# Between the heads and the MLP: the last block's projected outputs copied by ScalarE, and three row pairs' latent products ahead of the context

## The chip, the cores and the metric

One core of a Trainium2 chip. The metric is the device time of one execution in microseconds, as the median of several runs. All tensors are fp32 in HBM.

## What is computed

The reference is a two-layer diffusion trunk over 256 context and 1024 latent tokens of width 1024. Layer 0 mixes tokens with multi-head latent attention (MLA), layer 1 with gated linear attention (GLA). Cut to what matters here:

```python
y_lat = o_lat @ w_o                                   # projected heads (and y_ctx in layer 0)
x_lat = x_lat + m_lat[:, 2] * rms_norm(y_lat, g1)     # sandwich norm, residual
h     = modulate(rms_norm(x_lat, g2), m_lat[:, 3], m_lat[:, 4])
x_lat = x_lat + m_lat[:, 5] * rms_norm(square(relu(h @ w1)) @ w2, g3)
# in layer 0 the same for x_ctx, with its own modulation
```

The stretch of interest lies between `@ w_o` and the first products of `h @ w1`.

## The kernel before

The tokens are handled in three blocks: block 0 is the context (256 tokens), blocks 1 and 2 are the latents (512 each). The order of the blocks is `BLK_ORDER = (1, 0, 2)`, so block 2 is the last to get its projection. Activations lie transposed, 128 features by 512 (or 256) tokens in a tile, eight tiles for a block.

Each fp32 product is made of three rounded products. A factor is split into a high part, cast by ScalarE (ACT, L203), and a low part, source minus high part, mostly by VectorE (DVE, L200). The matmul of a pair of tiles is then high by high (L233), high by low (L234), low by high (L235). So nothing on TensorE (PE) can start before an ACT cast, nor its second matmul before a DVE subtraction.

`out_items` projects the heads of one block: two halves of four PSUM tiles; each tile is copied to SBUF (L809) and its square is summed (`sumsq`: square on ACT, L297 or L300; sum on DVE, L301). `residual_norm_steps` then makes the norm: `rstd` sums over the partitions with a matmul by ones (L308), does L314 to L316 on ACT and L317 to L319 on DVE; each tile is scaled (L857), the old stream, loaded by DMA, is added (L859), the sum is stored (L865) and its square summed; a second `rstd` follows, and then the modulated tiles (L877/L878 for latents; L325 on DVE, L327 on ACT as the high part, L328 on DVE as the low part for the context).

`mlp` multiplies by `w1` in a Strassen-like scheme. For a pair `p` of its row strips, `up_first` loads, casts and splits two weight tiles and makes two 4-step products with block 1's tiles (24 matmuls of 128x512; copy L971, sum L886, L965 and L966). `up_first_ctx` makes the context's two up-products for the same pair (24 matmuls of 128x256 each; the first with the two weights held from `up_first`, the second with two weights of its own; then L936 and L937). In layer 0 `PLAN["ahead"]` pairs get their `up_first` before the first `up_first_ctx`. The weights come out of a pool of 12 tiles (`w`), so three pairs of two weights, high and low, fill it.

Each engine's order is not the order of the code: a scheduler with a timeline of its own orders the instructions of the whole program, and every engine works its own queue off in that order. The ends of all this that matter here are the order rows under "The change".

Of the kernel before, what the change touches and what calls it, by code (L numbers as in the profile page):

```python
# [35 lines left out]
BLK_ORDER = (1, 0, 2)  # L36
# [43 lines left out]
           7: []},  # L80
 'pbufs': {'m': 56, 'c': 16, 'w': 12, 'stg': 12, 's': 4, 't': 7},
 'early': [8, 11],
 'ahead': 2,
 'etick': [10.0, 5.0],
 'fill': [[2, 1], [2, 1], [1, 1], [1, 1], [1, 1], [1, 1], [1, 1], [1, 1], [1, 0], [1, 0], [1, 0], [1, 0], [1, 0],
          [1, 0], [1, 1], [2, 1], [2, 2], [2, 2], [2, 2], [2, 3], [2, 2]],
# [21 lines left out]
class Trunk:  # L108
# [684 lines left out]
    def out_items(self, res, l, b, wname, src, off, xsrc):  # L793
        t0, w = BLK[b]
        acc = self.m(512)[:, :w]
        o, ys = [], []
        for half in range(2):
            pss = [self.ps(w) for _ in range(4)]
            for k in range(KT):
                if half == 0:  # L800
                    o.append(self.msplit(self.load(src[k, :, t0 - off:t0 - off + w]), w, self.nc.vector))
                ww = self.weight(self.I[wname][k * P:(k + 1) * P, half * 512:half * 512 + 512], self.nc.vector)
                for n in range(4):
                    self.mm3(pss[n], self.cols(ww, n * P), o[k], k == 0, k == KT - 1)
                self.tick(w * PLAN["tk"][0])
                yield
            for n in range(4):
                y = self.m(512)[:, :w]
                self.nc.vector.tensor_copy(y, pss[n])  # L809
                self.sumsq(acc, pss[n], half == 0 and n == 0, w)  # L810
                ys.append(y)
        self.bg.append(self.residual_norm_steps(res, l, b, ys, acc, xsrc, 2, (l, 4), (l, 3), b != 0))
# [870 lines left out]
```

## Time and profile before

| | |
|---|---|
| median of 3 runs | 2874.68 us (2873.05 to 2877.36) |
| the profiled execution | 2872.26 us, span of its trace 2870.5 us |
| mean granted TensorE clock | 0.98 of full speed |
| PE busy | 2747.0 us (96%) |
| DVE busy | 2280.4 us (79%) |
| ACT busy | 1594.9 us (56%) |

How to read it: the span is what the trace covers; the execution's own time is 1.8 us longer, and the median of the runs is 2.42 us above the profiled execution. An engine's row of a timeline gives the start in us from the span's start, the time in us, the line, the operation and its tiles; "x4" is a run of four; in brackets stands how long the engine had been idle before it and what released it. Runs of one engine overlap a little, as the next instruction begins before the last has drained.

### The profile page before, as it was taken

How to read it: one execution, taken by the hardware profiler on the slowest of the kernel's cores; microseconds unless marked ns; L12 is line 12 of the kernel's file. 1: busy time of each engine (PE TensorE's matmuls, PEld its weight loads, DVE VectorE, ACT ScalarE, POOL GpSimd, SP SyncE). 2: the span in 40 equal slices, each digit the busy share in tenths (PEclk: the TensorE clock that was granted, in tenths of full speed). 3: DMA queues.
4: the chain of work that ended last, by engine and by line, in shares of the span. 5: the costliest groups of instructions: out<-in, count | busy, mean ns of one | idle time of the engine just before them, and what ended most of it. 6: DMA issues, size and time to landing. Idle time of an engine off the chain costs nothing.

```text
span 2870.5 us, 44551 instructions
## 1 busy us (share of the span) xinstructions
PE 2747.0 (96%) x14774; PEld 2362.8 (82%) x14774; DVE 2280.4 (79%) x4303; ACT 1594.9 (56%) x3341; POOL 638.2 (22%) x464
## 2 busy tenths in 40 slices
PE   8999898999989999999999999999888999999997
PEld 6788887898779888888888888888786778888877
DVE  6898899887788887798868674476998998777766
ACT  4667576666566444444545456666655645554443
POOL 2554444422000000000002232566560000000022
PEclk9999999999999999999999999999999999999999
DMA  7122334323637675498745566776675767577454
GB/s 251 43 79 67 122 108 132 101 78 120 217 118 236 197 253 180 152 342 283 255 125 187 164 202 191 243 241 213 209 257 198 235 212 247 191 278 254 149 178 154
DMA packets 319529, 535.50 MB, mean 187 GB/s; under 512 B 33217, under 2 KB 96577, under 8 KB 319297
## 3 DMA queue, kind: packets, MB, share of 16 engines
q1 hardware_dynamic: 313472, 527.40, 55.6%
q10 hardware_dynamic: 5760, 5.25, 0.5%
q8 instruction: 116, 1.90, 0.3%
q14 instruction: 117, 0.95, 0.1%
q0 software_dynamic: 64, 0.00, 0.0%
HBM read 412.19 MB, written 120.32 MB: 186 GB/s over the span
## 4 chain that ended last, share of the span: by engine, by line
PE 75%; DVE 14%; ACT 4%; DMA 4%; issue 2%; POOL 1%; SPq 0%; DVEq 0%; ACTq 0%; POOLq 0%
PE ps L234 23%; PE ps L233 23%; PE ps L235 22%; DVE m L200 2%; PE ps L736 1%; DVE y L709 1%; DVE ada L252 1%; DMA stg<-hid 1%; PE ps L704 1%; ACT m L203 1%; PE ps L705 1%; PE ps L706 1%; PE ps L707 1%; PE ps L708 1%; PE ps L308 1%
## 5 line engine op out<-in xcount | busy, mean ns | idle before, releaser
L234 PE MATMUL ps<-m,w 128*128 128x512 f32 (+1 forms) x2320 | 895.8, 387 | 12.1 <-DVE m L200 11.4
L233 PE MATMUL ps<-m,w 128*128 128x512 f32 (+1 forms) x2320 | 880.7, 389 | 19.4 <-ACT m L203 15.3
L235 PE MATMUL ps<-m,w 128*128 128x512 f32 (+1 forms) x2320 | 887.9, 386 | 2.1 <-DVE w L200 2.1
L200 POOL TENSOR_TENSOR w<-stg,w 128x512 fp32r<-128x512 f32 (+2 forms) x138 | 197.6, 1435 | 1696.2 <-ACT w L203 1622.7
L233 PEld LDWEIGHTS ps<-m,w 128*128 128x128 f32 x2320 | 438.2, 190 | 111.9 <-ACT m L203 23.1
L234 PEld LDWEIGHTS ps<-m,w 128*128 128x128 f32 x2320 | 440.6, 190 | 104.3 <-DVE m L200 18.2
L235 PEld LDWEIGHTS ps<-m,w 128*128 128x128 f32 x2320 | 438.6, 190 | 90.9 <-DVE w L200 4.3
L203 ACT CAST w<-stg 128x512 fp32r<-128x512 f32 (+2 forms) x510 | 312.1, 616 | 318.2 <-PE ps L234 250.9
L200 DVE TENSOR_TENSOR w<-stg,w 128x512 fp32r<-128x512 f32 x372 | 273.2, 737 | 120.5 <-ACT w L203 109.6
L203 ACT CAST m<-stg 128x512 fp32r<-128x512 f32 x296 | 177.5, 625 | 142.5 <-DMA stg<-hid 127.0
L200 DVE TENSOR_TENSOR m<-stg,m 128x512 fp32r<-128x512 f32 x244 | 167.5, 699 | 47.9 <-ACT m L203 47.0
L234 PE MATMUL ps<-m,m 128*128 128x256 f32 (+1 forms) x632 | 197.3, 312 | 6.3 <-DVE m L200 4.0
L233 PE MATMUL ps<-m,m 128*128 128x256 f32 (+1 forms) x632 | 189.2, 316 | 13.0 <-DVE m L1531 6.8
L233 PE MATMUL ps<-c,w 128*128 128x256 f32 (+1 forms) x664 | 189.5, 289 | 12.3 <-ACT c L327 4.6
L235 PE MATMUL ps<-m,m 128*128 128x256 f32 (+1 forms) x632 | 193.6, 306 | 0.0
L234 PE MATMUL ps<-c,w 128*128 128x256 f32 (+1 forms) x664 | 187.4, 284 | 1.3 <-DVE c L432 1.3
L235 PE MATMUL ps<-c,w 128*128 128x256 f32 (+1 forms) x664 | 186.2, 285 | 0.0
L203 ACT CAST w<-m 128x512 fp32r<-128x512 f32 x128 | 79.2, 622 | 116.9 <-PE ps L234 116.7
L233 PEld LDWEIGHTS ps<-m,m 128*128 128x128 f32 x632 | 124.1, 198 | 22.6 <-DVE m L1531 7.7
L233 PEld LDWEIGHTS ps<-c,w 128*128 128x128 f32 x664 | 127.3, 193 | 17.4 <-ACT c L327 5.0
L886 DVE TENSOR_TENSOR t<-ps,t 128x512 f32<-128x512 f32 x164 | 111.0, 684 | 37.5 <-PE ps L235 31.6
L965 ACT ACTIVATE t<-t 128x512 f32<-128x512 f32 x109 | 68.7, 631 | 127.0 <-DVE t L886 120.2
(301 smaller groups left out, 5826.9 us busy)
## 6 DMA issues: line engine op xcount, KB each, us to landing
stg<-in_mlp_w SPq DMA_DIRECT2D x256, 256.0 KB, 4.3
stg<-hid SPq DMA_DIRECT2D x227, 256.0 KB, 3.9
hid<-t SPq DMA_DIRECT2D x205, 256.0 KB, 3.4
stg<-in_w SPq DMA_DIRECT2D x182, 256.0 KB, 3.4
ada<-in_adaT SPq DMA_DIRECT2D x80, 512.0 KB, 3.7
stg<-in_adaT SPq DMA_DIRECT2D x112, 256.0 KB, 4.2
stg<-in_gla_wv SPq DMA_DIRECT2D x64, 256.0 KB, 3.8
stg<-in_mla_wo SPq DMA_DIRECT2D x48, 256.0 KB, 4.4
```

Of the source, the lines that this page charges most:

```text
L200: eng.tensor_tensor(out=out, in0=a, in1=bits(hi), op=ALU.subtract)
L203: self.nc.scalar.copy(hi, src)
L233: mm(ps, lhs[0], rhs[0], start=first, stop=False, skip_group_check=shared)
L234: mm(ps, lhs[0], rhs[1], start=False, stop=False, skip_group_check=shared)
L235: mm(ps, lhs[1], rhs[0], start=False, stop=last, skip_group_check=shared)
L252: pin(nc.vector.tensor_tensor_reduce(out=w, in0=w, in1=self.cs[:, s], scale=1.0, scalar=0.0, op0=ALU.mult, op1=ALU.add, accum_out=c))
L308: nc.tensor.matmul(tot, self.ones, a, start=i == 0, stop=i == len(acc) - 1)
L704: mm(ps, qh[:, qs], kh, start=True, stop=False)
L705: mm(ps, qh[:, qs], kl, start=False, stop=False)
L706: mm(ps, ql[:, qs], kh, start=False, stop=False)
L886: eng.tensor_tensor(out=out, in0=a, in1=b, op=op)
L965: self.nc.scalar.activation(c, c, AF.Relu)
```

## The change

One number of `PLAN` and one line of `out_items`:

```diff
  'early': [8, 11],
- 'ahead': 2,
+ 'ahead': 3,
...
             for n in range(4):
                 y = self.m(512)[:, :w]
-                self.nc.vector.tensor_copy(y, pss[n])
+                (self.nc.scalar.copy if b == BLK_ORDER[-1] else self.nc.vector.tensor_copy)(y, pss[n])
                 self.sumsq(acc, pss[n], half == 0 and n == 0, w)
```

In layer 0 a third pair's products with block 1 come ahead of the context's up-products. In both layers the eight copies of block 2's projected tiles go from DVE to ACT: 16 instructions of 128x512. The numbers of instructions are otherwise the same; the scheduler orders all of them anew. Tile names below: `ps` are PSUM tiles, `m`, `c`, `t` SBUF tiles, `w` weights, `stg` freshly loaded weights; two numbers in a row are high and low part.

ACT, layer 0, from the last weight casts to the casts of block 1's tiles (`m_9914`, `m_9918`, ...). Before:

```order
L203 CAST w_10000<-stg_9998 128x512
L203 CAST w_10126<-stg_10124 128x512
L297 ACTIVATE m_9802<-m_9184 128x256
L300 ACTIVATE t_9814<-m_9187 128x256
L300 ACTIVATE t_9840<-m_9192 128x256
L300 ACTIVATE t_9848<-m_9197 128x256
L203 CAST w_10132<-stg_10130 128x512
L203 CAST m_9914<-m_9583 128x512
L203 CAST m_9918<-m_9610 128x512
L300 ACTIVATE t_9854<-m_9399 128x256
L203 CAST m_9922<-m_9613 128x512
```

and of the change:

```order
L809 COPY m_9903<-ps_9663 128x512
L203 CAST w_10046<-stg_10044 128x512
L809 COPY m_9908<-ps_9664 128x512
L203 CAST m_9914<-m_9583 128x512
L300 ACTIVATE t_9854<-m_9399 128x256
L300 ACTIVATE t_9860<-m_9404 128x256
L300 ACTIVATE t_9884<-m_9409 128x256
L203 CAST m_9918<-m_9610 128x512
L300 ACTIVATE t_9890<-m_9414 128x256
L300 ACTIVATE t_9895<-ps_9661 128x512
L300 ACTIVATE t_9900<-ps_9662 128x512
L300 ACTIVATE t_9905<-ps_9663 128x512
```

After these twelve rows comes the cast of `m_9922`. The four copies of the second half stand before the first cast of `m`, and seven squares between the first and the third cast, where one stood.

PE, layer 0, around the context's norm (`L308 ... 128x256`) and block 2's first one (`L308 ... 128x512`). Before:

```order
L235 MATMUL ps_10020<-m_9942,w_10001 128x512
L308 MATMUL ps_10038<-m_9802,ones 128x256
L233 MATMUL ps_10095<-c_10049,w_9948 128x256
L233 MATMUL ps_10136<-c_10049,w_10126 128x256
L308 MATMUL ps_10173<-m_9419,ones 128x512
L233 MATMUL ps_10182<-c_10049,w_9994 128x256
L234 MATMUL ps_10095<-c_10050,w_9948 128x256
```

and of the change:

```order
L235 MATMUL ps_10066<-m_9942,w_10047 128x512
L308 MATMUL ps_10084<-m_9802,ones 128x256
L233 MATMUL ps_10141<-c_10095,w_9948 128x256
L234 MATMUL ps_10141<-c_10096,w_9948 128x256
L235 MATMUL ps_10141<-c_10095,w_9949 128x256
...
L235 MATMUL ps_10141<-c_10137,w_9955 128x256
L233 MATMUL ps_10182<-c_10095,w_10172 128x256
L234 MATMUL ps_10182<-c_10096,w_10172 128x256
L308 MATMUL ps_10219<-m_9419,ones 128x512
L233 MATMUL ps_10228<-c_10095,w_9994 128x256
```

The third pair's product (`ps_10066` is its second half) stands ahead of the context's norm. The context's first up-product (`ps_10141`) runs through alone, 24 matmuls, before block 2's norm; before, three such products were interleaved from the start and the norm came third. Block 2's second norm has the same place in PE's queue in both programs (row 4421); between the two norms of block 2 stood 238 rows and stand 190 now.

DVE, layer 0, the end of the sum of squares (`m_10298`) that block 2's second norm waits for, of the change:

```order
L200 TENSOR_TENSOR w_10725<-stg_10722,w_10724 128x512
L886 TENSOR_TENSOR t_10436<-ps_10451,t_10435 128x512
L301 TENSOR_TENSOR m_10298<-m_10298,t_10402 128x512
L937 SCALAR_TENSOR_TENSOR t_10494<-ps_10469,t_10494 128x256
L301 TENSOR_TENSOR m_10298<-m_10298,t_10408 128x512
L937 SCALAR_TENSOR_TENSOR t_10535<-ps_10510,t_10535 128x256
L301 TENSOR_TENSOR m_10298<-m_10298,t_10414 128x512
L301 TENSOR_TENSOR m_10298<-m_10298,t_10420 128x512
```

The last two sums stand behind the L937 that reads `ps_10510`, the product whose last matmul is directly ahead of the second norm in PE's queue. Before, both of these L937 and this L200 came after the last sum.

## Rows read from the trace of the kernel before

**Rows 1.** The page: busy time, share and instructions; shares of the last chain.
```profile
PE 2747.0 (96%) x14774; PEld 2362.8 (82%) x14774; DVE 2280.4 (79%) x4303; ACT 1594.9 (56%) x3341; POOL 638.2 (22%) x464
...
PE 75%; DVE 14%; ACT 4%; DMA 4%; issue 2%; POOL 1%; SPq 0%; DVEq 0%; ACTq 0%; POOLq 0%
```

**Rows 2.** Windows: span, busy us by engine, then PEclk, DMA share, GB/s.
```profile
840.00:850.00 10.00, 5.35 (x19) 3.83 (x18) 7.43 (x18) 7.28 (x17) 0.00 (x0) 0.74 0.15 54
```

**Rows 3.** Timeline of PE, layer 0, from the first products to the context's.
```profile
828.14 1.22 PE L233 MATMUL ps<-m,w 128*128 128x512 f32 x2 [2.19 <-ACT m L203]
...
837.64 0.39 PE L235 MATMUL ps<-m,w 128*128 128x512 f32 x1
...
840.13 0.40 PE L235 MATMUL ps<-m,w 128*128 128x512 f32 x1
840.37 0.60 PE L308 MATMUL ps<-m,ones 128*128 128x256 f32 x2
845.61 0.80 PE L233 MATMUL ps<-c,w 128*128 128x256 f32 x2 [4.65 <-ACT c L327]
846.21 1.91 PE L308 MATMUL ps<-m,ones 128*128 128x512 f32 x2
...
848.13 0.41 PE L234 MATMUL ps<-c,w 128*128 128x256 f32 x1
...
851.33 0.41 PE L234 MATMUL ps<-c,w 128*128 128x256 f32 x1
...
851.84 0.28 PE L234 MATMUL ps<-c,w 128*128 128x256 f32 x1
851.96 0.28 PE L235 MATMUL ps<-c,w 128*128 128x256 f32 x1
```

**Rows 4.** Timeline of ACT in the same stretch.
```profile
824.78 1.13 ACT L203 CAST m<-m 128x512 fp32r<-128x512 f32 x2
...
835.12 1.20 ACT L971 COPY t<-ps 128x512 f32<-128x512 f32 x2
```

**Rows 5.** Timeline of DVE in the same stretch, to block 2's last sum.
```profile
831.28 2.49 DVE L200 TENSOR_TENSOR m<-m,m 128x512 fp32r<-128x512 f32 x4
833.69 3.83 DVE L301 TENSOR_TENSOR m<-m,t 128x512 f32<-128x512 f32 x8
...
843.15 0.42 DVE L317 SCALAR_TENSOR_TENSOR m<-m,c 128x256 f32<-128x256 f32 x1 [1.83 <-ACT c L316]
...
849.29 1.66 DVE L328 SCALAR_TENSOR_TENSOR c<-t,m,c 128x256 fp32r<-128x256 f32 x4
850.87 0.68 DVE L317 SCALAR_TENSOR_TENSOR m<-m,m 128x512 f32<-128x512 f32 x1
...
880.56 0.68 DVE L301 TENSOR_TENSOR m<-m,t 128x512 f32<-128x512 f32 x1
```

**Rows 6.** Timeline of PE: block 2's second norm.
```profile
883.09 1.02 PE L308 MATMUL ps<-m,ones 128*128 128x512 f32 x2
```

**Rows 7.** Lines of DVE, 850.8 to 881.9: busy, mean ns, idle before.
```profile
L200 DVE TENSOR_TENSOR w<-stg,w 128x512 fp32r<-128x512 f32 x13 | 8.7, 683 | 1.0 <-ACT w L203 1.0
...
L859 DVE TENSOR_TENSOR m<-m,s 128x512 f32<-128x512 f32 x8 | 5.4, 687 | 2.0 <-DMA s<-in_xT 1.8
```

**Rows 8.** All waits of PE, 845 to 1000: total us, times, longest.
```profile
PE ps L233 <- ACT c L327: 4.6, 1, 4.6
```

**Rows 9.** The copies by line: duration in ns, min/median/max.
```profile
L809 DVE COPY m<-ps x32: 414/679/692, 722.8 to 2217.8; 128x512 f32<-128x512 f32 x24, 128x256 f32<-128x256 f32 x8
...
L971 ACT COPY t<-ps x32: 565/577/588, 835.1 to 2522.5; 128x512 f32<-128x512 f32 x32
```

**Rows 10.** Timeline of PE, layer 1, from the projection to block 2's second norm.
```profile
2216.40 0.50 PE L233 MATMUL ps<-m,w 128*128 128x512 f32 x1 [1.26 <-ACT m L203]
2219.75 0.50 PE L234 MATMUL ps<-m,w 128*128 128x512 f32 x1 [2.85 <-DVE m L200]
...
2256.78 1.12 PE L308 MATMUL ps<-m,ones 128*128 128x512 f32 x2 [1.57 <-DVE m L301]
```

## Prediction before the changed kernel ran

> **What bounds the kernel.** I read the page first: PE is busy 96% of the span, and PE makes up 75% of the chain that ended last, DVE 14%, ACT 4% [rows 1]. A change that leaves PE's matmuls as they are can only move its idle time, so I looked for PE's waits where the order changes. In layer 0 the windows show one bad stretch: 840 to 850 with PE busy 5.35 of 10 us and a granted clock of 0.74 [rows 2]. PE's timeline says why: the context's norm starts at 840.37, and the context's first product, which needs the normed and modulated tiles from ACT and DVE, only at 845.61, 5.24 us later, 4.65 of them idle [rows 3]. After that PE has no wait at all until 1000 [rows 8]. So time lost by PE in this stretch is not made up by anything behind it: there is no later idle time to absorb a delay. The second fact is what stands behind the cover: from block 2's first norm on PE (846.21) to its second (883.09) [rows 3, 6], PE works without a pause, but DVE needs nearly as long, from 850.87 to the end of the last sum of squares at 881.24 [rows 5]. The slack is 883.09 - 881.24 = 1.85 us. Whatever delays the start of that DVE chain, or takes PE work out of that stretch, shows as idle time of PE.
>
> **The copies.** A copy takes 679 ns on DVE and 577 on ACT [rows 9]; eight go over per layer. A DVE instruction of 512 follows the last at about 0.60 us (four L200 in 2.49) [rows 5], an ACT copy too (two in 1.20) [rows 4]. DVE is rid of 4.8 us per layer, ACT gets as much. What counts is where they stand: before the casts that PE waits for. ACT's first cast of block 1's tiles came at 824.78 [rows 4]; by the order of the change the four copies of the second half stand ahead of it, which partly takes the place of other squares, and I put it at 826. To the third cast lie, by that order, two casts, four squares of 256 and three of 512; at 0.6 and 0.3 us that is 4.2 us, so the third cast starts at 830.2, ends at 830.8, and its subtraction ends at 831.5. Before, PE ran through from 828.14 [rows 3]. It would now have done some eight matmuls by 831.5. Before, 48 products ended at 840.37, and twelve of them from 837.64 to 840.13 are 0.226 apart [rows 3]; so 9 were done by 831.5. The delay is 0.2 us, and up to 1.5 more if PE's clock rises only after that; with two more copies' worth (1.2) ahead of the casts it is 3. I take 2.
>
> **The third pair.** 24 matmuls of 0.226 us, 5.4 in all, are moved ahead, and the context's norm stands behind them in PE's queue, though its input is complete at 837.52 (the eight sums from 833.69 take 3.83 us [rows 5]). So they cover nothing: the norm starts at 840.37 + 5.4 + 2 = 847.8, and the 5.24 us to the first context product stay. That starts at 853.0.
>
> There the second effect sets in. All 12 weight tiles hold the three pairs' weights, so the weights for the context's second product cannot be cast before its first (24 matmuls) has read the last of its own. Before, three such products were interleaved while the low parts came in, and block 2's norm went third. Now one product runs alone, at the pace of the low parts: the first low matmul came 2.52 us after the start (848.13), the last low part 5.3 us after it (849.29 + 1.66 = 850.95 against 845.61); 15 steps from 848.13 to 851.33 took 0.213 each, later ones 0.12 [rows 3, 5]. The product ends 5.8 us (low parts alone) to 7.4 us (2.5 + 23 x 0.213) after its start; I take 6.6, and 0.4 for the two matmuls behind it. **Block 2's norm on PE is then at 860.0**, 13.8 us later than before.
>
> **The DVE chain.** From there the chain takes three terms. From norm to L317: 2.8 us, as for the context (840.37 to 843.15); it took 4.66 for block 2 [rows 3, 5]. DVE's work: before 30.4 us from 850.87 to 881.24, less 3.0 of idle (1.0 for a weight's cast, 2.0 for the old stream's DMA [rows 7]), so 27.4. By the order of the change two more weight subtractions and one L937 stand before the last sum and one L886 less: 1.2 + 0.35 - 0.6, so 28.3. Idle: 0 at best; at worst the cast and the DMA cost twice as much, 6; I take 3.5, near what was measured. So the second norm is at 860.0 + 2.8 + 28.3 + 3.5 = 894.6, **11.5 us later than 883.09** [rows 6]. The matmuls done by then are the same ones: the norm has kept its place in PE's queue. PE has in this stretch 24 x 0.226 + 166 x 0.12 = 25.4 us of work for 34.6 us, so about 9 us are idle, in several waits. The ends: without idle time on DVE and with the short product and front, 6 later; with the long ones, 16. Then the clock: after the one wait of 4.65, PE ran at half its pace until 851.3 [rows 3], so part of a second such loss is likely; I add 0.7.
>
> **Layer 1.** Here only the copies change. PE waits 1.26 and 2.85 us at the first products and 1.57 at block 2's second norm [rows 10]. ACT now has the copies between the last modulations and the first cast; I put that cast 2.4 us (four copies) later, which PE gets back in part, as fewer products stand between and the last wait goes. Sum +1, with ends -4.4 (2.85 and 1.57 both vanish) and +3.
>
> **Sum.** 11.5 + 0.7 + 1.0 = 13.2 on the profiled execution's 2872.26 us, so 2885.5; the median shown is 2.42 above that execution, so 2887.9.
>
> **Rivals.** (a) *The relief of DVE wins.* The low parts and sums come 2.4 us earlier per half, PE's waits on DVE's subtractions (2.85) and on DVE's sum (1.57) [rows 10] go, and in layer 0 DVE's chain keeps up. That gives -4 to -5, so about 2870. For it: copies on ACT are 0.1 us shorter each [rows 9], and DVE is the busier engine (79 against 56%) [rows 1]. Against it: both first waits are named after ACT's casts [rows 10], which the copies now precede. [...]
>
> (b) *The third product does cover the wait.* 5.4 us of products against 4.65 idle: were the context's norm taken up ahead of them, most of the 4.65 would go, and the time be about 2870 to 2871. The order speaks against it, since the norm stands behind the product's last matmul.
>
> (c) *The delays cancel.* If the DVE chain has no new idle time and PE's stretch is refilled, only the front's 2 and a lag of 1 or so from the lone product stay, less what layer 1 gains: +1 to +4, so 2876 to 2879. For it: the scheduler fitted the order to a timeline of its own. Against: DVE needed 30.4 of the 36.9 us before, and now has fewer matmuls beside it.
>
> (d) *It is worse.* The old stream's loads stand on SP's queue behind a store that needs the context's second product, which is late now; if they land late, and the clock drops again at each wait, 18 to 20 are lost: 2893 to 2895.
>
> (e) *The change doesn't do what it says*, that is, the scheduler undoes it: excluded by the order rows.
>
> **Chances.** My forecast 0.57, (a) 0.06, (b) 0.04, (c) 0.21, (d) 0.12. A measurement here can tell about 0.2%, 5.7 us, from no change. Faster by more takes (a) or (b) at their best: 0.09. (c) and the low end of the forecast (+6) are within it: 0.19. Slower: 0.72. The range: below, the edge of (c) with layer 1's gain, 2872; above, (d) with its upper end plus the median's offset, 2897.
>
> **What would show it.** In the changed profile: the four ACT copies ahead of the first cast, whose row says 826; the context's norm after 72 products, near 848, with an idle time of 4 to 5 us behind it; 24 context matmuls alone, then block 2's norm near 860; in the windows from 860 to 895 several waits of PE on weights (DVE L200) and one for L301 at the second norm near 895; no idle time after that. The forecast is wrong if the context's norm has no wait behind it, if PE is busy throughout from 855 to 890, or if layer 1 moves by more than 4 us.

## The result, and the profile after

The changed kernel takes 2890.51 us (median of 6 runs, 2881.69 to 2895.07), the kernel before 2875.50 (6 runs, 2873.05 to 2878.61): 15.0 us slower. The ratio of the runs is 1.0057, 95% interval 1.0043 to 1.0070, which on 2875.5 is 12 to 20 us. Forecast were 2887.9, range 2872 to 2897, with slower at 0.72. The profiled execution took 2891.31 us, its span 2889.5.

Up to the context's first norm in layer 0 (L308, 128x256, at 812.93 before and at 810.11 now) PE's order is the same in both, and executions are up to 6 us apart there for no reason of the change. I therefore count times in layer 0 from this norm. PE's timeline of the changed kernel (start us, us, engine, line, operation, idle before):

```profile
810.11 0.60 PE L308 MATMUL ps<-m,ones 128*128 128x256 f32 x2
...
823.59 0.50 PE L233 MATMUL ps<-m,w 128*128 128x512 f32 x1 [1.97 <-ACT m L203]
825.82 0.79 PE L234 MATMUL ps<-m,w 128*128 128x512 f32 x1 [1.73 <-DVE m L200]
...
829.57 0.80 PE L234 MATMUL ps<-m,w 128*128 128x512 f32 x1 [0.82 <-DVE m L200]
...
834.00 0.63 PE L233 MATMUL ps<-m,w 128*128 128x512 f32 x1
834.43 0.53 PE L234 MATMUL ps<-m,w 128*128 128x512 f32 x1
834.80 0.40 PE L235 MATMUL ps<-m,w 128*128 128x512 f32 x1
...
846.87 0.60 PE L308 MATMUL ps<-m,ones 128*128 128x256 f32 x2
852.12 0.58 PE L233 MATMUL ps<-c,w 128*128 128x256 f32 x1 [4.65 <-ACT c L327]
854.35 0.58 PE L234 MATMUL ps<-c,w 128*128 128x256 f32 x1 [1.65 <-DVE c L328]
859.31 1.02 PE L308 MATMUL ps<-m,ones 128*128 128x512 f32 x2
...
892.68 2.07 PE L308 MATMUL ps<-m,ones 128*128 128x512 f32 x2 [7.19 <-DVE m L301]
```

From the first norm to the context's second one: 36.8 us now, 27.4 before; to block 2's first: 49.2 against 33.3; to block 2's second: 82.6 against 70.2 [rows 3, 6]. So 12.4 us are lost by there. The row of 4.65 is the same as before to the hundredth: the third product covered nothing. The row of 7.19 is new. PE's waits between 800 and 900 (who waited for whom: us in all, times, longest), where before there were 4.6 for ACT's L327 and 3.2 for ACT's L203:

```profile
PE ps L308 <- DVE m L301: 7.2, 1, 7.2
PE ps L233 <- ACT c L327: 4.7, 1, 4.7
PE ps L234 <- DVE m L200: 2.6, 2, 1.7
PE ps L233 <- ACT m L203: 2.0, 1, 2.0
PE ps L234 <- DVE c L328: 1.6, 1, 1.6
```

In sum they are 18.0 us against 7.8. So 10.2 of the 12.4 us are waits, and the other 2.2 are matmuls that ran at a lower pace.

DVE's lines from 862 to 892.7, the stretch that answers to [rows 7]:

```profile
L200 DVE TENSOR_TENSOR w<-stg,w 128x512 fp32r<-128x512 f32 x14 | 9.4, 687 | 0.3 <-ACT w L203 0.2
...
L859 DVE TENSOR_TENSOR m<-m,s 128x512 f32<-128x512 f32 x8 | 5.3, 686 | 1.0 <-DMA s<-in_xT 1.0
...
L317 DVE SCALAR_TENSOR_TENSOR m<-m,m 128x512 f32<-128x512 f32 x1 | 0.7, 692 | 1.6 <-ACT m L316 1.6
L886 DVE TENSOR_TENSOR t<-ps,t 128x512 f32<-128x512 f32 x1 | 0.7, 691 | 0.9 <-DMA hidc<-t 0.9
```

In the 30 us from L317 (862.41) on, DVE is idle for 2.1 us only: it is the engine that sets block 2's second norm, as forecast, and PE waits for it. The ACT rows at the front:

```profile
822.42 0.60 ACT L809 COPY m<-ps 128x512 f32<-128x512 f32 x1
822.89 0.64 ACT L203 CAST m<-m 128x512 fp32r<-128x512 f32 x1
...
825.52 1.56 ACT L300 ACTIVATE t<-ps 128x512 f32<-128x512 f32 x3
826.95 0.63 ACT L203 CAST m<-m 128x512 fp32r<-128x512 f32 x1
```

The first cast comes 12.8 us after the norm (before 11.9), the third 16.8 (before 13.2, by this row of the kernel before):

```profile
826.14 0.60 ACT L203 CAST m<-m 128x512 fp32r<-128x512 f32 x1
```

The windows of the changed kernel, to be held against [rows 2]:

```profile
830.00:840.00 10.00, 10.00 (x35) 8.03 (x35) 3.73 (x7) 1.25 (x3) 0.00 (x0) 0.76 0.07 26
...
850.00:860.00 10.00, 6.24 (x29) 5.63 (x29) 8.25 (x21) 4.89 (x11) 0.00 (x0) 0.66 0.13 45
...
890.00:900.00 10.00, 7.32 (x23) 5.29 (x24) 5.65 (x11) 3.74 (x8) 0.00 (x0) 0.69 0.52 194
```

In the stretches with the waits, or right behind them, the granted clock is below 1 (0.76, 0.66 and 0.69): after the waits at the front, PE's matmuls stand 0.43 apart until 834.4, where later ones stand 0.226 apart. I call this half pace: the granted clock is 0.56 from 823 to 834.4 and 0.97 from there to 840; before, it is 0.68 from 826 to 831 and 0.98 from there to 836.

### The profile page after: what moved, and what is told of

Its sections match the earlier page's. It is cut to its first block, busy times and chain, and to the rows that moved or that the text cites. A ratio compares the mean times of both kernels' runs of the same rounds, so it can differ in the third digit from the quotient of the medians.

```text
span 2889.5 us, 44540 instructions
## 1 busy us (share of the span) xinstructions
PE 2754.2 (95%) x14774; PEld 2366.7 (82%) x14774; DVE 2274.9 (79%) x4287; ACT 1600.7 (55%) x3357; POOL 635.5 (22%) x464
## 4 chain that ended last, share of the span: by engine, by line
PE 50%; DVE 7%; DMA 3%; ACT 2%; issue 2%; SPq 0%; POOL 0%; DVEq 0%; ACTq 0%; POOLq 0%
PE ps L234 16%; PE ps L235 16%; PE ps L233 16%; DVE m L200 1%; DVE m L886 1%; DVE t L886 1%; DVE w L200 1%; DMA stg<-hid 0%; ACT m L203 0%; DVE m L301 0%; DVE m L857 0%; DMA stg<-in_gla_wr 0%; PE ps L308 0%; DVE m L1570 0%; DMA stg<-in_gla_wo 0%
## 5 line engine op out<-in xcount | busy, mean ns | idle before, releaser
L233 PE MATMUL ps<-m,w 128*128 128x512 f32 (+1 forms) x2320 | 885.1, 391 | 25.3 <-ACT m L203 19.0
L200 POOL TENSOR_TENSOR w<-stg,w 128x512 fp32r<-128x512 f32 (+2 forms) x138 | 196.0, 1423 | 1720.0 <-ACT w L203 1648.4
L203 ACT CAST w<-stg 128x512 fp32r<-128x512 f32 (+2 forms) x510 | 311.6, 615 | 294.3 <-PE ps L234 229.5
L200 DVE TENSOR_TENSOR w<-stg,w 128x512 fp32r<-128x512 f32 x372 | 274.1, 740 | 126.8 <-ACT w L203 115.4
L203 ACT CAST m<-stg 128x512 fp32r<-128x512 f32 x296 | 177.5, 624 | 143.1 <-DMA stg<-hid 122.8
L200 DVE TENSOR_TENSOR m<-stg,m 128x512 fp32r<-128x512 f32 x244 | 165.9, 692 | 44.0 <-ACT m L203 42.7
L886 DVE TENSOR_TENSOR t<-ps,t 128x512 f32<-128x512 f32 x164 | 111.0, 684 | 43.8 <-PE ps L235 34.3
L203 ACT CAST w<-m 128x512 fp32r<-128x512 f32 x128 | 79.2, 622 | 119.5 <-PE ps L234 119.3
L233 PEld LDWEIGHTS ps<-m,m 128*128 128x128 f32 x632 | 123.9, 197 | 25.3 <-DVE m L1531 6.4
```

The source lines that it names most:

```text
L200: eng.tensor_tensor(out=out, in0=a, in1=bits(hi), op=ALU.subtract)
L203: self.nc.scalar.copy(hi, src)
L233: mm(ps, lhs[0], rhs[0], start=first, stop=False, skip_group_check=shared)
L886: eng.tensor_tensor(out=out, in0=a, in1=b, op=op)
```

## The experiments

Four questions: is layer 0's loss the third pair's or the copies'; what of the third pair makes it (the place of the norm, the full weight tiles, DVE's chain); does layer 1 lose by its copies; and can the wait of 4.65 be won. The table gives, from the traces, the time from the context's first norm in layer 0 to its second norm and to block 2's two norms, and the whole time against before.

| run | context's 2nd | block 2's 1st | block 2's 2nd | median us | ratio, 95% |
|---|---|---|---|---|---|
| before | 27.4 | 33.3 | 70.2 | 2874 to 2876 | |
| the change | 36.8 | 49.2 | 82.6 | 2890.5 | 1.0043 to 1.0070 |
| x1 third pair only | 32.9 | 45.7 | 77.7 | 2889.4 | 1.0027 to 1.0055 |
| x2 copies only | 25.5 | 34.3 | 70.5 | 2883.2 | 1.0017 to 1.0037 |
| x3 copies in layer 1 only | 28.8 | 34.6 | 70.7 | 2878.3 | 0.9991 to 1.0016 |
| x4 x1, norm ahead of third product | 27.5 | 37.6 | 71.1 | 2882.1 | 1.0010 to 1.0036 |
| x5 x1, 16 weight tiles, 8 staging | 32.5 | 38.1 | 74.3 | 2925.2 | 1.0155 to 1.0194 |
| x6 x1, 8 staging | 33.2 | 45.2 | 77.5 | 2927.5 | 1.0162 to 1.0204 |
| x7 the change, copies in layer 0 only | 36.9 | 49.4 | 82.9 | 2894.6 | 1.0051 to 1.0077 |
| x8 before, norm ahead of 2nd product | 26.0 | 32.2 | 68.2 | 2877.3 | 0.9992 to 1.0009 |
| x9 the change, sums on GpSimd | 36.9 | 49.4 | 80.9 | 2893.0 | 1.0047 to 1.0075 |
| x10 x8, sums on GpSimd | 25.8 | 32.1 | 68.3 | 2879.4 | 1.0007 to 1.0032 |
| x11 the change, first half's copies only | 32.7 | 45.6 | 77.7 | 2889.2 | 1.0038 to 1.0065 |
| x12 x10, context's sums too | 20.5 | 29.1 | 65.7 | 2877.6 | 1.0000 to 1.0026 |

**x1: the third pair alone.** `'ahead': 3`, copies on DVE.

> Three pairs ahead, copies on DVE as before. My theory: layer 0 loses by the third pair alone (the context's norm stands behind its product, its 12 weight tiles are full, so block 2's norm comes late and the DVE chain to its second norm is left uncovered): block 2's second norm on PE at 891 to 896 against 883, layer 1 as before, in all 10 to 12 us slower than before. Rival 1, the copies on ACT make the loss in both layers: at most 3 us slower. Rival 2, the order is merely disturbed everywhere: a loss spread over the span, with no single stretch of 8 us.

Block 2's second norm is 7.6 us later than before, with the same 4.65 behind the context's norm and a wait of 5.80 at block 2's second:

```profile
845.56 0.60 PE L308 MATMUL ps<-m,ones 128*128 128x256 f32 x2
...
850.81 0.39 PE L233 MATMUL ps<-c,w 128*128 128x256 f32 x1 [4.65 <-ACT c L327]
...
890.43 2.07 PE L308 MATMUL ps<-m,ones 128*128 128x512 f32 x2 [5.80 <-DVE m L301]
```

The context's second norm is 5.4 later, the product's 24 x 0.226. In all the ratio is 1.0041 (about 12 us). So 7.6 of the change's 12.4 us in layer 0 are the third pair's; the delay at the front, beyond its 24 matmuls, is not.

**x2 and x3: the copies.**

```diff
+                (self.nc.scalar.copy if b == BLK_ORDER[-1] else self.nc.vector.tensor_copy)(y, pss[n])
```

x2 has this with `'ahead': 2`, x3 with `and l == 1` added.

> Copies of block 2 on ACT in both layers, two pairs ahead as before. In this order the context's norm stands 26 matmuls ahead of the end of the two products. My theory: layer 0 gains (the 5.2 us between norm and first context product are covered by those 26 matmuls, 26 x 0.226 = 5.9 us; less 2 us for the later casts): 2 to 4 us faster at block 2's second norm; layer 1 loses 5 to 7; in all 1 to 5 slower. Rival 1 (the copies make the loss in both layers): 10 or more slower.

> Copies on ACT in layer 1 only, two pairs ahead. My theory: layer 0 and the scan as before; the first cast of block 1's tiles comes later behind the copies, PE waits 6 us at layer 1's first products where it waited 4.1, and block 2's second norm comes 4 to 6 later; 4 to 7 slower in all. Rival 2 (disturbance of the order in the scan makes layer 1's loss): within 2 us of before, as the scan's order is that of before.

In x2 the scheduler moved the context's norm ahead of 26 matmuls, and the wait behind it fell from 4.65 to 1.9; yet block 2's second norm is no earlier (+0.4). The gain that I expected did not come: taken 26 matmuls (5.9 us) earlier, the context's norm should have come 21.5 us after the first one and came at 25.5, so the front is 4.0 us late here as in the change. x2 is slower by 1.0027 all the same, so it loses elsewhere, in stretches that I did not follow up. x3 does not bear out my theory for layer 1: no measurable loss. PE waited 5.38 us once at layer 1's first products where it had waited 1.26 and 2.85, and the wait of 1.57 at block 2's second norm [rows 10] was gone.

**x4: the norm ahead of the third product.** x1 with

```diff
-        held = [self.up_first(l, p, ops) for p in range(ahead)]
+        held = []
+        for p in range(ahead):
+            if p == 2:
+                self.ready(h[0])
+            held.append(self.up_first(l, p, ops))
```

> Three pairs ahead, copies on DVE, but the context's norm is emitted before the third pair, and stands ahead of its product in PE's queue. My theory: the wait of 4.65 for the context's first tile is covered by the third product's 24 matmuls (5.4 us), so 4 to 5 us come back against the third pair alone; the full weight tiles and the DVE chain still cost, so 4 to 8 slower than before. If instead the wait behind the norm does not count because the DVE chain to the second norm sets the end: no better than the third pair alone by more than 2.

6.65 us come back at block 2's second norm (71.1 against 77.7), of the 7.6 that the third pair cost there. PE's waits from the first norm to there fall from 15.5 to 11.0 us in sum, as the 4.65 is gone; the other 2.1 are pace, since the matmuls are the same ones. The place of the norm in PE's queue is the third pair's main cost in this stretch. But DVE's chain then sets the end:

```profile
878.46 2.08 PE L308 MATMUL ps<-m,ones 128*128 128x512 f32 x2 [6.32 <-DVE m L301]
```

**x5 and x6: the weight tiles.** x1 with `'w': 16, 'stg': 8`, and its control with `'w': 12, 'stg': 8` (8 staging tiles in both, to make room for the 16).

> Three pairs ahead, copies on DVE, but 16 weight tiles (and, for room, 8 staging tiles instead of 12). In this order block 2's norm goes third behind the context's norm, as before the change. My theory (full weight tiles push block 2's norm behind a lone product): norm to norm 6 us or so again, block 2's first norm at 851 to 853 instead of 858.4, the second at 883 to 887, the wait for the last sum gone or under 3. Rival (the lone product is only the wait for the context's tiles, whatever the weights): first norm at 856 or later, the second as in the third pair alone, 890.

> Control for the run with 16 weight tiles: three pairs ahead, copies on DVE, 12 weight tiles, 8 staging tiles. If the staging tiles matter little, block 2's norms as with the third pair alone (858 and 890); what it is slower in all than the third pair alone is the price of the smaller staging.

Fewer staging tiles cost some 38 us in the whole program, so only this stretch is compared. In x5 PE's timeline reads as the kernel before does:

```profile
845.49 0.60 PE L308 MATMUL ps<-m,ones 128*128 128x256 f32 x2
850.74 0.50 PE L233 MATMUL ps<-c,w 128*128 128x256 f32 x2 [4.65 <-ACT c L327]
851.07 1.62 PE L308 MATMUL ps<-m,ones 128*128 128x512 f32 x2
```

Block 2's first norm is 5.6 us behind the context's instead of 12.0 in x6, and stands behind 2 matmuls in PE's queue instead of 26: the full weight tiles do make the lone product. But of the 7.1 us that the first norm came sooner only 3.2 arrived at the second (74.3 against 77.5), where PE still waited 5.4 us for the last sum.

**x7: the change without layer 1's copies.** `and l == 0` added.

> The change with the copies on ACT in layer 0 only. Up to layer 1's projection the order is that of the change. Theory now: layer 1's copies cost 3 to 5 us in the change's own order (block 2's second norm there came 91.4 us after the mean of the earlier norm's L308, against 87.9), so this is 3 to 5 faster than the change and the stretch takes 88. Rival: that difference is scatter between executions, and this is within 2 of the change.

It is no faster than the change (2894.6 against 2890.5). The stretch takes 89.0 us, and PE waits there without the copies too:

```profile
2236.07 0.79 PE L234 MATMUL ps<-m,w 128*128 128x512 f32 x1 [5.24 <-DVE m L200]
...
2274.59 1.13 PE L308 MATMUL ps<-m,ones 128*128 128x512 f32 x2 [2.37 <-DVE m L301]
```

So the 3.5 us that the change's profile shows in that stretch (2182.4 to 2273.8 between two norms, before 2168.9 to 2256.8) can't be put down to the copies: without them it takes 87.1 to 90.6 in x1, x4, x7 and x8, with them 87.2 and 87.8 in x2 and x3. No cost of layer 1's copies shows; one of a few us is not excluded, as x3's interval reaches up to 4.6.

**x8: the kernel before with its norm ahead.** As x4, with `'ahead': 2` and `p == 1`.

> The kernel before, only with the context's norm emitted ahead of the second pair's products: two pairs, 12 weight tiles, copies on DVE. Theory: the wait of 4.65 behind the norm was the part of this stretch that can be won, and 24 products (5.4 us) cover it, with no lone product behind: context's first product at 840 to 841, block 2's second norm 4 to 5 earlier (878 to 879 against 883), 3 to 5 faster in all. Rival: block 2's DVE chain then sets the end, its second norm waits for the last sum, and no more than 2 are won.

The rival held. The wait of 4.65 is gone, but two waits for sums take its place, the first at the context's norm itself:

```profile
838.08 0.70 PE L308 MATMUL ps<-m,ones 128*128 128x256 f32 x2 [2.12 <-DVE m L301]
```

The second is 1.49 at block 2's second norm. Of 4.65 only 1.9 are won there, and in all nothing shows (1.0000; the interval would still allow the 1.9). In x8's profile the 1.9 are gone at the next norm (704.1 us after the first one, before 701.3). Most of that is lost between 1290 and 1360, where the order of PE is that of before and the DMA engines' share is much the same (0.84 from 1300 to 1350, before 0.83). From 1290 to 1400 PE waits in x8

```profile
PE ps L235 <- DVE w L200: 2.8, 6, 0.8
```

for the low parts of weights, 1.0 before. But this is not shown to be the price of coming early: x7 and x11 come there 14 and 10 us later than the kernel before, counted from the first norm, and wait 2.9 and 3.0 for the same low parts.

**x9, x10, x12: the sums on GpSimd**, which is idle in this stretch.

```diff
-                self.sumsq(acc2, ys[k], k == 0, w)
+                self.sumsq(acc2, ys[k], k == 0, w, nc.gpsimd if (l, b, gate) == (0, 2, 2) else None)
```

This is x9's and x10's line; in x12 the condition is `l == 0 and gate == 2 and b != 1`, which takes in the context. The three expectations follow in the order x9, x10, x12; x12's "run before last but one" is x10.

> The change, with the seven sums of squares of block 2's second norm in layer 0 taken off DVE and put on GpSimd, which is idle there. Theory: DVE's work between block 2's norms (28 us for 25 us of PE's) sets the second norm; seven sums of 0.6 less shorten it by up to 4.2, less one GpSimd sum of 1.2 at the end: second norm 2 to 4 us after the first one sooner (29.5 to 31.5 instead of 33.4), its wait 4 to 5 instead of 7.2, in all 2 to 4 faster than the change. Rival: GpSimd's sums (1.2 to 1.5 each, eight in a row behind late DMAs) end no sooner, or slow DVE: no gain.

> The kernel before with the context's norm ahead of the second pair's products, and block 2's sums on GpSimd. Theory: with the 4.65 covered, DVE's chain was next (waits of 3.6 in all for sums); with the sums on GpSimd the wait at block 2's second norm (1.5) goes: 2 to 4 us faster than before. Rival: no gain over the norm ahead alone.

> As the run before last but one, with the context's sums on GpSimd too. Theory: the wait of 2.1 at the context's norm for its last DVE sum is shortened as well: 3 to 6 us faster than the kernel before. Rival: eight GpSimd sums in a row take longer than DVE's, the context's norm comes later, and it is no faster than before.

x9: block 2's two norms lie 31.5 us apart instead of 33.4. Seven sums less on DVE should have given up to 4.2; the second norm now waits for GpSimd's last sum:

```profile
891.25 2.07 PE L308 MATMUL ps<-m,ones 128*128 128x512 f32 x2 [5.33 <-POOL m L301]
```

GpSimd's seven sums follow each other from 876.74 to 891.20, 14.46 us in all, as these sums and DVE's instructions took longer beside each other (below). In all nothing is gained. x10 gains nothing over x8 (68.3 against 68.2, and 1.0007 to 1.0032 in all). x12 wins 4.5 us at block 2's second norm, the most of all, and still is not faster (1.0000 to 1.0026). Not all of the 4.5 need be the sums': in x12 the context's norm also stands 11 matmuls further ahead in PE's queue than in x10. Where they are lost again I did not trace; from 1290 to 1400 PE waits 3.0 us for weights, as in x7 and x11. No version beat the kernel before.

**x11: the change with the second half's copies back on DVE.** `and half == 0` added.

> The change with the four copies of each projection's second half back on DVE; the first half's four stay on ACT. Theory: it is the second half's four copies, ahead of the first casts, that delay the front: the context's norm comes 5.4 us after that of before (as with the third pair alone) instead of 8.9, block 2's second norm 3 to 4 earlier than in the change, in all 2 to 5 faster than the change. Rival: the first half's copies delay the weight casts as much: no difference.

The context's norm comes 32.7 us after the first, as with the third pair alone, and block 2's second at 77.7, 4.8 less than in the change. So the second half's four copies, ahead of the casts, are the whole of the copies' cost up to there; the first half's cost nothing that shows. Of these 4.8 only 1.3 show in the medians, whose intervals are wide enough for either.

## Why the prediction was right, and where it was off

- **Nothing to cover.** Right. The context's norm stood behind the third product, the 4.65 stayed to the hundredth, x4 won them back with the norm's place.
- **The front.** Mechanism right, size wrong: the term "I take 2" measured 3.9 (36.76 - 27.44 - 5.42), above the upper end of 3 that I gave. ACT's casts came no later than I had said: the first at 12.8 us after the norm (826 would be 13.1), the third at 16.8 (830.2 would be 17.3). But the third tile's subtraction on DVE then stood behind five of the context's sums,

```profile
826.62 2.29 DVE L301 TENSOR_TENSOR m<-m,t 128x256 f32<-128x256 f32 x5
828.83 0.68 DVE L200 TENSOR_TENSOR m<-m,m 128x512 fp32r<-128x512 f32 x1
```

  and its low part was used 0.9 us later than I had worked out (829.57 - 810.11 = 19.5 after the norm, against 831.5 - 812.9 = 18.6). The larger part is the clock, 0.56 from 823 to 834.4. PE's waits at the front grew from 3.2 only to 4.5; the other 2.6 of the 3.9 are pace: PE ran at half pace until 834.4, 24.3 after the norm, where before it had done so to 831, 18 after it. I had put that clock loss at up to 1.5 and taken less. x11 shows that the second half's four copies make all of the 3.9.
- **The lone product.** Block 2's first norm was forecast 12.2 us after the context's (860.0 - 847.8) and came 12.4 after it. x5 shows the cause, the full weight tiles, and what I had not said: of its cost only 3.2 us reach the second norm.
- **The DVE chain.** 34.6 forecast, 33.4 measured: to L317 3.1 (2.8), the work 28.1 (28.3), idle 2.1 (3.5). PE did not wait in several places, as I wrote, but once, for 7.2 us, at the second norm. Its own work in this stretch took 26.2, forecast 25.4 (24 x 0.226 + 166 x 0.12 is 25.3).
- **Layer 0 in sum.** +12.4 at the second norm, forecast +11.5. An undersized front (by 1.9) and an oversized idle time of DVE (by 1.4) partly cancel, so it is in part luck that the sum came so near. The clock's term behind it, 0.7 in the forecast, measured 1.8: the norm itself runs at half pace (two L308 in 2.07 instead of 1.02; granted clock 0.50 from 893 to 896), and PE's twentieth matmul behind it begins 6.7 us after it, before 5.0. With it 14.2 of the 15.0 us are accounted for. Further on nothing can be told: to the next norm, some 630 us on, it takes 632.7 against 631.1, and x3, whose order there is that of before, takes 632.8.
- **Layer 1.** The term +1, with ends -4.4 and +3, is not contradicted; x3 gives between -3 and +5 for the copies there, so its size is not settled, and a near sum says nothing for it. The profile shows waits of 5.13 and 1.01 at the first products,

```profile
2232.85 0.79 PE L233 MATMUL ps<-m,w 128*128 128x512 f32 x1 [5.13 <-ACT m L203]
...
2235.80 0.79 PE L233 MATMUL ps<-m,w 128*128 128x512 f32 x1 [1.01 <-ACT m L203]
...
2273.83 1.12 PE L308 MATMUL ps<-m,ones 128*128 128x512 f32 x2 [2.29 <-DVE m L301]
```

  so the second norm's wait, which I let go, did not go in the change's own order. x7, without the copies there, has nearly the same waits.
- **The rivals.** (a) fell: the relief of DVE won nothing in layer 0, where PE waited at the front for a later ACT cast (1.97) and then for DVE's subtractions all the same (1.73 and 0.82). The copies took less time each, 594 ns in the median on ACT in the changed kernel against 679 on DVE before [rows 9], but what stood behind them waited. Nor are both of layer 1's first waits named after ACT's casts, as I wrote: the 2.85 is named after DVE's L200 [rows 10]. (b) fell for the change, as the norm stands behind the product; x4 shows that its mechanism works once the norm stands ahead. (c) fell: the delays added up. Of (d) half came: the clock was low again behind the waits (granted 0.76, 0.66 and 0.69 in the windows above), but the old stream's loads were not late (DVE idle 1.0 for them, before 2.0). The sentence "there is no later idle time to absorb a delay" held for the change. Whether a gain in this stretch reaches the end stays open: x12's 4.5 us do not show in its median.

What stays open: why x2 is 8 us slower with layer 0 unchanged at the second norm, why x12's gain is lost, and what layer 1's copies cost, if anything. Profiled executions in which a long stretch has the same order differ by 2 to 4 us, as x7 and the change do up to layer 1. From layer 0's second norm to the end, x3's profile is 8.8 us longer than that of before, though their medians agree, and the change's is 9.4 longer: so I attribute nothing that lies there.

## What to carry to other kernels

Moving work ahead of a wait covers it only if the instruction that starts the way to what ends the wait (here the context's norm) is queued before that work on the same engine (x1 kept the wait of 4.65, x4 lost it); read the queue, not the amount of work. When two chains run side by side with little slack (36.9 us on PE, 35.0 on DVE here), starting both later with less work on the one side turns the difference into idle time (7.19 us here). And a copy moved to the less busy engine is not free if the cast that everything waits for is queued behind it there (4.8 us here, by x11). What the waits cost here is more than their length: 2.6 of the 3.9 us at the front were the half pace behind them.

## What the runs showed of the hardware that I had not expected

GpSimd's sums and DVE's additions and subtractions of two SBUF tiles took longer beside each other. In x9, GpSimd's timeline, its first sum and a later pair:

```profile
876.74 4.34 POOL L301 TENSOR_TENSOR m<-m,t 128x512 f32<-128x512 f32 x1 [185.26 <-ACT t L300]
...
887.93 3.27 POOL L301 TENSOR_TENSOR m<-m,t 128x512 f32<-128x512 f32 x2
```

and DVE's beside it:

```profile
876.83 1.30 DVE L859 TENSOR_TENSOR m<-m,s 128x512 f32<-128x512 f32 x2
...
883.26 5.15 DVE L859 TENSOR_TENSOR m<-m,s 128x512 f32<-128x512 f32 x3
888.33 3.42 DVE L200 TENSOR_TENSOR w<-stg,w 128x512 fp32r<-128x512 f32 x2
891.67 0.68 DVE L886 TENSOR_TENSOR t<-ps,t 128x512 f32<-128x512 f32 x1
```

While DVE ran on with hardly a pause, GpSimd's first sum took 4.34 us, where three of its size in the kernel before, between 18.5 and 47.4, took 1.27 to 1.31 (it ended at 881.08; DVE's first pause of more than 0.1 us, 0.64 long, ended at 880.91); when GpSimd's sums followed each other at 1.6 to 1.7, DVE's additions and subtractions of two SBUF tiles took 1.7 each, in step with them, where eight L859 took 0.69 in the median in the changed kernel, with GpSimd idle. In x10, DVE's L886, which reads one tile from PSUM, kept its 0.68 in the middle of three of GpSimd's sums:

```profile
864.18 1.79 DVE L200 TENSOR_TENSOR w<-stg,w 128x512 fp32r<-128x512 f32 x1
865.90 0.68 DVE L886 TENSOR_TENSOR t<-ps,t 128x512 f32<-128x512 f32 x1
```

though GpSimd's three ran from 863.66 to 868.50 without a gap. The two DVE instructions on two SBUF tiles that began within them took 1.79 and 1.69. What holds the one engine up beside the other no run shows. DVE was relieved of up to 4.2 us in x9 (seven sums at 0.6); 1.9 arrived at the norm, less than half.
